# Low parts by an accumulating DMA, and four seven-product pairs in every group, in a two-layer encoder trunk

## The chip, the cores and the metric

The kernel runs on one core of a Trainium2 chip. The metric is the device time of one execution in microseconds; a run's figure is the median of several executions. Each kernel also leaves a profile of one execution, with every engine's instructions, what they waited for, and the DMA queues.

The core has a matrix engine (TensorE, "PE" in the profile), three engines for elementwise work (VectorE "DVE", ScalarE "ACT", GpSimd "POOL"), and SyncE ("SP"), which here issues nearly all loads. Each engine works through its own instructions in order.

## The reference, cut to what matters

The program is a trunk of two layers on 256 tokens of width 2048, in float32. Each layer has attention and a squared-ReLU MLP with 8192 hidden features:

```python
def sq_relu_mlp(h, g, w_in, w_out):
    return jnp.square(jax.nn.relu(rms_norm(h, g) @ w_in)) @ w_out

for layer in range(DEPTH):                 # DEPTH = 2
    ...
    h = h + jnp.concatenate([y_main, y_mem], axis=-1) @ w_o[layer]
    h = h + sq_relu_mlp(h, norm_mlp[layer], w_mlp_in[layer], w_mlp_out[layer])
```

The change touches only the second product of the MLP, the down projection: (256 x 8192) times (8192 x 2048), in both layers.

## The kernel before, in words

**Two parts of each number.** A float32 product is made of three matmuls in the engine's rounded 32-bit format (fp32r). Each operand is split into a high part, which is its rounding, and a low part, which is the rest; then high x high, high x low and low x high are added in PSUM. For weights the high part is a cast on ScalarE and the low part a subtraction on VectorE (`parts`, L173 and L176).

**Units.** All weights stream through the kernel as units of 128 x 1024 values (512 KB), in one list `stream` whose order is the order of their use. `prepare` takes the next unit: it gets a raw tile, a high tile and a low tile, loads raw with a DMA from SP, and makes the two parts. The pools hold 6 raw, 4 high and 5 low tiles. `weights` keeps up to four units prepared ahead of the one that the matmuls take. Matmuls are issued in program order; for the other engines a planner, which goes by its own costs, sets the order of the instructions within an engine.

**The MLP.** Hidden features are worked in four chunks of 2048. A chunk has an up stage (16 tiles of features, 32 units) and then down projections by tokens. In chunks 0 to 2 the 2048 output columns are covered by two pair groups of 1024 columns each; in chunk 3 by one pair group and two plain groups of 512 columns (the last of layer 1 is done by features). That is 7 pair groups a layer, 14 in all.

**A pair group** (`pair_group`) has 8 pairs of feature tiles j. A pair is a 2 x 2 block product: two halves of the tokens, two tiles of features, two sides of 512 output columns. It is done in one of two ways.

- Direct: one unit for the left side and one for the right (`Gathered`, steps "1" and "2"), each with 4 block products of 3 matmuls, 24 for the pair. The DMA gathers the unit from four rows of the weight's layout, so raw has the order (o, k, n), with o one of four runs of 128 output columns and k the feature tile. The cast (L249) and the subtraction (L250) turn it to (k, o, n), so that a matmul reads 512 columns in one run.
- By seven products (`Sevenfold`, steps 0 to 3): the scheme of Winograd and Strassen, with 7 block products instead of 8, 21 matmuls of 512 columns for the pair. Its two raw tiles stay until the fourth step; VectorE forms sums of weight blocks in place (L222, L223, L225, L226), the cast is L227 and the subtraction L228. The sums on the token side (`factors`) are made at the end of a feature tile in the up stage (`finish`, L1111 to L1125).

`SEVEN[layer][chunk][group]` says which pairs go by seven products: 9 of the 14 groups have four such pairs (0, 2, 4, 6), and 5 have three (0, 2, 4). `group_order` lays the direct units between the steps. With four seven-product pairs the order of a pair is: step 0, step 1, a direct unit, step 2, a direct unit, step 3. The group then has 8 direct units; with three it has 10.

The two plain groups of chunk 3 take `Gathered` units too (24 of them over both layers); they go through `tile_by_tokens`.

POOL does the low part of the hidden activations (L1095), some sums of squares and other small work; before the change it issues no DMA of weights.

Of the kernel before, what the change touches and what calls it, by code (L numbers as in the profile page):

```python
# [9 lines left out]
F32 = mybir.dt.float32  # L10
F32R = mybir.dt.float32r
AF = mybir.ActivationFunctionType
ALU = mybir.AluOpType
# [29 lines left out]
WARM_UP = 10  # L43


THREE, FOUR = (0, 2, 4), (0, 2, 4, 6)
SEVEN = [
    [(FOUR, FOUR), (THREE, FOUR), (THREE, FOUR), (THREE,)],
    [(FOUR, FOUR), (THREE, FOUR), (THREE, FOUR), (FOUR,)],
]  # L50


def group_order(sevens):
# [13 lines left out]
class InOrder:  # L67


    def __init__(self, tc, engine):  # L70
        self._tc, self._engine = tc, engine
# [10 lines left out]
class Gathered:  # L82


    def __init__(self, ap):
        self.ap = ap


class Sevenfold:
# [16 lines left out]
def trunk(  # L106
# [17 lines left out]
    nc = Engines(tc)  # L124
# [21 lines left out]
    for _ in range(WARM_UP):  # L146
# [9 lines left out]
        out=neg_tri[:], in_=neg_ones[:], pattern=[[-1, P]], compare_op=ALU.is_ge,  # L156
# [9 lines left out]
    stream = []  # L166
    prepared = deque()
    state = {"next": 0}

    def parts(raw, hi, lo, shared=False):  # L170

        n = 256 if shared else raw.shape[-1]
        nc.scalar.copy(hi[:, :n], raw[:, :n])  # L173
        if shared:
            nc.vector.tensor_copy(hi[:, n:], raw[:, n:])
        nc.vector.tensor_tensor(lo, raw, hi.bitcast(F32), op=ALU.subtract)  # L176
# [55 lines left out]
    def prepare():  # L232
        i = state["next"]
        if i >= len(stream):
            return
        state["next"] = i + 1
        if isinstance(stream[i], Sevenfold):
            prepare_seven(i, stream[i])
            return
        raw = raws.tile([P, 1024], F32, name=f"raw{i}", tag="raw")  # L240
        hi = his.tile([P, 1024], F32R, name=f"hi{i}", tag="hi")
        lo = los.tile([P, 1024], F32R, name=f"lo{i}", tag="lo")
        if isinstance(stream[i], Gathered):

            nc.sync.dma_start(raw[:].rearrange("p (o x) -> p o x", o=4), stream[i].ap)
            turned = raw[:].rearrange("p (o k n) -> p k o n", o=4, k=2)
            hi4 = hi[:].rearrange("p (k o n) -> p k o n", o=4, k=2)
            lo4 = lo[:].rearrange("p (k o n) -> p k o n", o=4, k=2)
            nc.scalar.copy(hi4, turned)  # L249
            nc.vector.tensor_tensor(lo4, turned, hi4.bitcast(F32), op=ALU.subtract)  # L250
            prepared.append((hi, lo))
            return
        nc.sync.dma_start(raw[:], stream[i])
        parts(raw[:], hi[:], lo[:])
        prepared.append((hi, lo))
# [33 lines left out]
    def mm(o, lhs, rhs, start, stop):  # L289
        nc.tensor.matmul(o, lhs, rhs, start=start, stop=stop)  # L290

    width = {"last": "narrow"}

    def tile_by_tokens(banks, act, unit, k2, kt, early=False):
        hi, lo = unit
        h512 = hi[:, k2 * 512 : (k2 + 1) * 512]
        l512 = lo[:, k2 * 512 : (k2 + 1) * 512]
        steps = []
        for m in range(2):
            a_hi = act[:, kt, m * P : (m + 1) * P]  # L300
            a_lo = act[:, kt, T + m * P : T + (m + 1) * P]

            steps.append((0, banks[m][:], a_hi, h512, kt == 0, False))
            steps.append((2, banks[m][:], a_hi, l512, False, False))
            steps.append((1, banks[m][:], a_lo, h512, False, kt == KT - 1))
        if early:

            steps.sort(key=lambda step: step[0])
        for step in steps:
            mm(*step[1:])  # L310
# [492 lines left out]
    def mlp_stream(l):  # L803
        for c in range(NCH):
            n = FIRST_UP if c == 0 else 0
            for h in range(2):
                for f in range(n):
                    stream.append(w_up[l, c * KT + f, h])
            for f in range(n, KT):
                for h in range(2):  # L810
                    stream.append(w_up[l, c * KT + f, h])
            def unit(g, j):
                ap = w_down[l, 4 * g : 4 * g + 4, 2 * c + j // 4]
                ap = ap[:, :, 256 * (j % 4) : 256 * (j % 4) + 256]
                return ap.rearrange("o p x -> p o x")

            for n, sevens in enumerate(SEVEN[l][c]):
                for j, step in group_order(sevens):
                    sides = [unit(2 * n + i, j) for i in range(2)]
                    if step == 0:  # L820
                        seven = Sevenfold(*sides)
                    stream.append(Gathered(sides["12".index(step)]) if step in ("1", "2") else seven)
            for g in range(2, 4) if c == NCH - 1 else ():
                if by_features(l, c, g):
                    for o in range(4 * g, 4 * g + 4):
                        for h in range(2):
                            stream.append(w_down[l, o, 2 * c + h])
                    continue
                stream.extend(Gathered(unit(g, j)) for j in range(KT // 2))
# [141 lines left out]
    def mlp(l, xg_, sq, h, done):  # L971
# [52 lines left out]
        def pair_group(c, n, hid, factors, staged=None):  # L1024

            banks = {q: ps_mm.tile([P, 512], F32, name="acc", tag="acc") for q in ("11", "21", "12", "22")}
            banks.update((q, ps_s.tile([P, 512], F32, name="acc", tag="s")) for q in ("p1", "p5"))
            banks["p6"] = ps_t.tile([P, 512], F32, name="acc", tag="t")
            banks["p7"] = ps_y.tile([P, 512], F32, name="acc", tag="y")
            sevens = len(SEVEN[l][c][n])  # L1030
            counts = {q: [0, 3 * sevens] for q in banks}
            for q in ("11", "21", "12", "22"):
                counts[q][1] = 6 * (KT // 2 - sevens) + (3 * sevens if q != "22" else 0)

            sums_of = {
                "11": [summed(0, 2 * n)], "21": [summed(1, 2 * n)],
                "12": [summed(0, 2 * n + 1)], "22": [summed(1, 2 * n + 1)],
                "p1": [product_sum(0, n), summed(0, 2 * n)], "p6": [product_sum(0, n)],
                "p5": [product_sum(1, n)], "p7": [product_sum(2, n)],
            }  # L1040

            def add(q, a, w):
                product(banks[q], a, w, counts[q])
                if counts[q][0] < counts[q][1]:
                    return
                src = banks[q][:]
                if staged is not None and q in ("12", "22", "p1", "p5", "p6", "p7"):

                    copy = wide.tile([P, 512], F32, name="copy", tag="wide")
                    nc.scalar.copy(copy[:], src)  # L1050
                    staged.extend((dst, copy[:]) for dst in sums_of[q])
                    return
                for dst in sums_of[q]:
                    if c == 0 and q not in ("11", "p6"):
                        nc.scalar.copy(dst, src)
                    else:
                        nc.vector.tensor_tensor(dst, src, dst, op=ALU.add)

            def tokens(kt, m):
                return [hid[:, kt, i * T + m * P : i * T + (m + 1) * P] for i in range(2)]  # L1060

            def part(unit, k2):
                return [x[:, k2 * 512 : (k2 + 1) * 512] for x in unit]

            for j, step in group_order(SEVEN[l][c][n]):
                w = weights()
                if step in ("1", "2"):
                    for m in range(2):
                        for k2 in range(2):
                            add(f"{m + 1}{step}", tokens(2 * j + k2, m), part(w, k2))  # L1070
                    slot()
                    continue
                s = factors[j]
                pairs = [
                    (("p1", tokens(2 * j, 0)), ("11", tokens(2 * j + 1, 0))),
                    (("12", s[3]),),
                    (("p5", s[0]), ("p7", s[2])),
                    (("p6", s[1]), ("21", tokens(2 * j + 1, 1))),
                ][step]
                for k2, (q, a) in enumerate(pairs):  # L1080
                    add(q, a, part(w, k2))
                if step in (1, 3):
                    slot()

        began = clock["slot"]
        for c in range(NCH):
# [4 lines left out]
            def finish(f, hid=hid, squares=squares, factors=factors, c=c):  # L1091
# [5 lines left out]
                )  # L1097
                if f % 2 == 0 or f // 2 not in SEVEN[l][c][-1]:
                    return
# [46 lines left out]
            n = FIRST_UP if c == 0 else 0  # L1146
# [60 lines left out]
            for g in range(2, 4):  # L1207
# [3 lines left out]
                for o in range(4 * g, 4 * g + 4):  # L1211
                    if o == KT - 1:
                        last_tile(
                            hid, lambda b, o=o: down_early(o, b), lambda b, o=o: down_last(o, b)
# [183 lines left out]
```

## Time and profile before

| | before |
|---|---|
| median of 3 runs | 2166.65 us (2166.62 to 2167.13) |
| the profiled execution: span from first to last instruction | 2165.4 us |
| TensorE busy | 2158.2 us |
| VectorE busy | 1690.1 us |
| ScalarE busy | 1191.3 us |
| POOL busy | 326.7 us |
| read from memory | 410.58 MB, 191 GB/s over the span |
| SP's queue: packets' share of 16 DMA engines | 62.0% |

The profiled execution has no time of its own beside its span; the span is 1.25 us under the median of the runs. In rows of groups, the columns are line, engine, operation, output and inputs, shapes and count, then busy time and mean duration in ns, then the idle time of the engine before them and what ended it. In rows of the timeline, the first two numbers are the start and the length in us. Matmuls overlap in the pipeline, so their single durations are longer than the distance between them.

### The profile page before, as it was taken

How to read it: one execution, taken by the hardware profiler on the slowest of the kernel's cores; microseconds unless marked ns; L12 is line 12 of the kernel's file. 1: busy time of each engine (PE TensorE's matmuls, PEld its weight loads, DVE VectorE, ACT ScalarE, POOL GpSimd, SP SyncE). 2: the span in 40 equal slices, each digit the busy share in tenths (PEclk: the TensorE clock that was granted, in tenths of full speed). 3: DMA queues.
4: the chain of work that ended last, by engine and by line, in shares of the span. 5: the costliest groups of instructions: out<-in, count | busy, mean ns of one | idle time of the engine just before them, and what ended most of it. 6: DMA issues, size and time to landing. Idle time of an engine off the chain costs nothing.

```text
span 2165.4 us, 30280 instructions
## 1 busy us (share of the span) xinstructions
PE 2158.2 (100%) x11083; PEld 1852.1 (86%) x11083; DVE 1690.1 (78%) x2431; ACT 1191.3 (55%) x1668; POOL 326.7 (15%) x349
## 2 busy tenths in 40 slices
PE   9999999999999999999999999999999999999999
PEld 8888888888888888888888889888888888988887
DVE  7778885678977987997886556567797798799796
ACT  7744545555655555555555447655565556555553
POOL 0010112621001001001050112352100100100100
PEclk9999999999999999999999999999999999999999
DMA  9655556655765765666666654455676577667665
GB/s 325 197 165 185 168 179 195 198 192 166 212 205 178 208 213 178 194 219 189 202 180 191 185 190 136 131 188 183 182 201 224 164 203 223 188 180 219 190 180 156
DMA packets 213317, 414.66 MB, mean 191 GB/s; under 512 B 13232, under 2 KB 144304, under 8 KB 213168
## 3 DMA queue, kind: packets, MB, share of 16 engines
q1 hardware_dynamic: 212592, 410.63, 62.0%
q8 instruction: 87, 1.43, 0.3%
q10 hardware_dynamic: 576, 2.10, 0.3%
q14 instruction: 62, 0.51, 0.1%
HBM read 410.58 MB, written 2.10 MB: 191 GB/s over the span
## 4 chain that ended last, share of the span: by engine, by line
PE 98%; DVE 1%; DMA 0%; issue 0%; ACT 0%; SPq 0%
PE acc L77 94%; PE yp L77 1%; PE accs L77 1%; PE tp L77 1%; PE s L77 1%; PE z L77 1%; DMA raw<-in_w_mem 0%; DVE lo L176 0%; DVE pt L640 0%; DVE lo L250 0%; DVE h L998 0%; ACT hi L173 0%; DVE kvx L465 0%; ACT hi L249 0%; PE stat L77 0%
## 5 line engine op out<-in xcount | busy, mean ns | idle before, releaser
L176 DVE TENSOR_TENSOR lo<-raw,hi 128x1024 fp32r<-128x1024 f32 (+1 forms) x524 | 642.6, 1237 | 308.4 <-ACT hi L173 183.3
L173 ACT CAST hi<-raw 128x1024 fp32r<-128x1024 f32 (+1 forms) x524 | 546.4, 1045 | 375.8 <-PE acc L77 316.7
L77 PE MATMUL acc<-hi,hid 128*128 128x512 f32 x1474 | 481.4, 389 | 0.0
L77 PE MATMUL acc<-mlpx,hi 128*128 128x512 f32 x2048 | 472.6, 390 | 0.0
L77 PEld LDWEIGHTS acc<-mlpx,hi 128*128 128x128 f32 x2048 | 382.0, 188 | 77.7
L77 PEld LDWEIGHTS acc<-hi,hid 128*128 128x128 f32 x1474 | 276.7, 188 | 57.5
L77 PE MATMUL acc<-lo,hid 128*128 128x512 f32 x737 | 286.7, 389 | 0.0
L1095 POOL TENSOR_TENSOR hid<-upsq,hid 128x256 fp32r<-128x256 f32 x128 | 122.3, 964 | 1086.2 <-ACT hid L1094 1086.2
L227 ACT CAST hi<-raw 128x1024 fp32r<-128x1024 f32 x204 | 192.1, 946 | 132.8 <-PE acc L77 56.0
L77 PEld LDWEIGHTS acc<-mlpx,lo 128*128 128x128 f32 x2048 | 250.6, 192 | 2.8
L77 PE MATMUL acc<-mlpx,lo 128*128 128x256 f32 x2048 | 252.0, 283 | 0.0
L228 DVE TENSOR_TENSOR lo<-raw,hi 128x1024 fp32r<-128x1024 f32 x204 | 222.8, 1108 | 29.6 <-ACT hi L227 28.0
L249 ACT CAST hi<-raw 128x1024 fp32r<-128x1024 f32 x146 | 154.0, 1055 | 126.1 <-PE acc L77 104.5
L77 PE MATMUL acc<-hi,xg 128*128 128x512 f32 x640 | 208.4, 398 | 0.0
L250 DVE TENSOR_TENSOR lo<-raw,hi 128x1024 fp32r<-128x1024 f32 x146 | 179.2, 1228 | 14.4 <-ACT hi L249 13.7
L77 PEld LDWEIGHTS acc<-lo,hid 128*128 128x128 f32 x737 | 138.4, 188 | 28.5
L77 PEld LDWEIGHTS acc<-hi,xg 128*128 128x128 f32 x640 | 120.2, 188 | 24.6
L451 ACT COPY low<-acc 128x256 f32<-128x256 f32 x188 | 69.1, 368 | 112.2 <-PE acc L77 111.9
L77 PE MATMUL acc<-lo,xg 128*128 128x512 f32 x320 | 124.7, 390 | 0.7 <-DVE lo L176 0.7
L77 PE MATMUL acc<-y,hi 128*128 128x512 f32 x512 | 119.9, 391 | 0.0
L77 PEld LDWEIGHTS acc<-y,hi 128*128 128x128 f32 x512 | 95.0, 188 | 19.0
L1094 ACT CAST hid<-upsq 128x256 fp32r<-128x256 f32 x128 | 51.9, 407 | 75.6 <-DVE upsq L1093 75.4
(202 smaller groups left out, 2610.4 us busy)
## 6 DMA issues: line engine op xcount, KB each, us to landing
raw<-in_w_up SPq DMA_DIRECT2D x256, 512.0 KB, 4.4
raw<-in_w_down SPq DMA_DIRECT2D x256, 512.0 KB, 5.6
raw<-in_w_in SPq DMA_DIRECT2D x80, 512.0 KB, 3.7
raw<-in_w_o SPq DMA_DIRECT2D x64, 512.0 KB, 4.0
raw<-in_w_mem SPq DMA_DIRECT2D x28, 512.0 KB, 5.9
raw<-in_w_kv_v SPq DMA_DIRECT2D x24, 512.0 KB, 3.9
raw<-in_w_kv_k SPq DMA_DIRECT2D x24, 512.0 KB, 4.2
raw<-in_w_q SPq DMA_DIRECT2D x24, 512.0 KB, 4.1
```

Source lines behind the costliest of these rows:

```text
L77: return self._tc.keep_in_program_order(fn(*args, **kwargs))
L173: nc.scalar.copy(hi[:, :n], raw[:, :n])
L176: nc.vector.tensor_tensor(lo, raw, hi.bitcast(F32), op=ALU.subtract)
L227: nc.scalar.copy(hi4, src)
L228: nc.vector.tensor_tensor(lo4, src, hi4.bitcast(F32), op=ALU.subtract)
L249: nc.scalar.copy(hi4, turned)
L250: nc.vector.tensor_tensor(lo4, turned, hi4.bitcast(F32), op=ALU.subtract)
L451: nc.scalar.copy(low[:], bank[:, T:])
L1094: nc.scalar.copy(hid[:, f, :T], a[:])
L1095: nc.gpsimd.tensor_tensor(hid[:, f, T:], a[:], hid[:, f, :T].bitcast(F32), op=ALU.subtract)
```

## The change

Direct units of the pair groups carry a mark, `by_dma`. Their low part isn't made by VectorE: ScalarE writes the rounding of -raw into the low tile, and a DMA issued from POOL adds raw onto it in place (512 KB from raw, accumulated into the low tile). The sum is raw minus the high part. `Gathered` units of the two plain groups in chunk 3 keep the subtraction on VectorE.

All `Gathered` units, marked or not, are no longer turned when they are split: high and low tiles keep the order (o, k, n), and the matmul reads its 512 columns as four runs of 128 (`turned`, `of_k`).

All 14 groups now have four seven-product pairs, so five groups exchange a direct pair for a seven-product pair. Their order of steps is then that of the other groups.

```diff
-THREE, FOUR = (0, 2, 4), (0, 2, 4, 6)
-SEVEN = [
-    [(FOUR, FOUR), (THREE, FOUR), (THREE, FOUR), (THREE,)],
-    [(FOUR, FOUR), (THREE, FOUR), (THREE, FOUR), (FOUR,)],
-]
+FOUR = (0, 2, 4, 6)
+SEVEN = [[(FOUR, FOUR), (FOUR, FOUR), (FOUR, FOUR), (FOUR,)] for _ in range(2)]
...
-    def __init__(self, ap):
+    def __init__(self, ap, by_dma=False):
         self.ap = ap
+        self.by_dma = by_dma
...
             nc.sync.dma_start(raw[:].rearrange("p (o x) -> p o x", o=4), stream[i].ap)
-            turned = raw[:].rearrange("p (o k n) -> p k o n", o=4, k=2)
-            hi4 = hi[:].rearrange("p (k o n) -> p k o n", o=4, k=2)
-            lo4 = lo[:].rearrange("p (k o n) -> p k o n", o=4, k=2)
-            nc.scalar.copy(hi4, turned)
-            nc.vector.tensor_tensor(lo4, turned, hi4.bitcast(F32), op=ALU.subtract)
-            prepared.append((hi, lo))
+            nc.scalar.copy(hi[:], raw[:])
+            if stream[i].by_dma:
+                nc.scalar.activation(lo[:], raw[:], AF.Copy, scale=-1.0)
+                nc.gpsimd.dma_start(out=lo[:].bitcast(F32), in_=raw[:], accum_op=ALU.add)
+            else:
+                nc.vector.tensor_tensor(lo[:], raw[:], hi[:].bitcast(F32), op=ALU.subtract)
+            turned = [x[:].rearrange("p (o k n) -> p k o n", o=4, k=2) for x in (hi, lo)]
+            prepared.append(turned)
             return
...
+    def of_k(x, k2):
+
+        return x[:, k2] if len(x.shape) == 4 else x[:, k2 * 512 : (k2 + 1) * 512]
...
-                    stream.append(Gathered(sides["12".index(step)]) if step in ("1", "2") else seven)
+                    stream.append(
+                        Gathered(sides["12".index(step)], True) if step in ("1", "2") else seven
+                    )
...
             def part(unit, k2):
-                return [x[:, k2 * 512 : (k2 + 1) * 512] for x in unit]
+                return [of_k(x, k2) for x in unit]
```

More of the change, by code (lines that the diff above doesn't have):

```diff
@@ L292, in trunk @@
     width = {"last": "narrow"}
+    def of_k(x, k2):
+        return x[:, k2] if len(x.shape) == 4 else x[:, k2 * 512 : (k2 + 1) * 512]
     def tile_by_tokens(banks, act, unit, k2, kt, early=False):
         hi, lo = unit
-        h512 = hi[:, k2 * 512 : (k2 + 1) * 512]
-        l512 = lo[:, k2 * 512 : (k2 + 1) * 512]
+        h512, l512 = of_k(hi, k2), of_k(lo, k2)
         steps = []
```

## The prediction

> **What bounds the kernel now.** I read the page first: busy shares and the chain that ended last.
>
> ```profile
> span 2165.4 us, 30280 instructions
> PE 2158.2 (100%) x11083; PEld 1852.1 (86%) x11083; DVE 1690.1 (78%) x2431; ACT 1191.3 (55%) x1668; POOL 326.7 (15%) x349
> ...
> PE 98%; DVE 1%; DMA 0%; issue 0%; ACT 0%; SPq 0%
> ```
>
> The chain is PE, 98% of it, and PE is without work for only 2165.4 - 2158.2 = 7.2 us. The span stands 1.25 us under the median of the runs (2166.65), so what I work out on the span carries over to the median.
>
> Then the waits of PE alone, and one piece of the chain with nothing but 512-wide products.
>
> ```profile
> PE tp L77 <- DVE h L998: 1.9, 2, 1.1
> PE cold L77 <- DVE zeros L144: 1.1, 1, 1.1
> PE acc L77 <- DVE lo L176: 0.7, 1, 0.7
> PE accs L77 <- ACT hi L173: 0.4, 1, 0.4
> ```
>
> ```profile
> 31.56 2.72 PE acc L77 x12
> ```
>
> No down projection unit is waited for today, and one 512-wide matmul costs 2.72 / 12 = 0.2267 us of PE's time (the longer durations of single matmuls overlap).
>
> Next the first two pair groups of layer 0 and the up stage behind them (PE, PEld, DVE, ACT, POOL busy, clock, DMA share, GB/s).
>
> ```profile
> 524.79:565.60 40.81, 40.81 (x182) 33.80 (x181) 39.20 (x47) 26.27 (x33) 2.95 (x2) 1.00 0.75 203
> 565.60:606.40 40.80, 40.80 (x182) 33.80 (x181) 36.90 (x41) 26.58 (x32) 0.00 (x0) 1.00 0.72 210
> 606.40:697.50 91.10, 91.10 (x524) 80.64 (x523) 67.81 (x107) 49.22 (x75) 12.44 (x15) 1.00 0.59 185
> ```
>
> A group with four seven-product pairs has 4 x 21 + 4 x 24 = 180 matmuls, and 180 x 0.2267 = 40.8 us: exactly its length. So even where VectorE is busy 36.9 of 40.8 us (90%), PE loses nothing to it. Relief of VectorE is worth nothing here by itself; what is left to win is the number of matmuls.
>
> **The part that gains.** Five groups go from three seven-product pairs to four (layer 0: one each in chunks 1, 2 and 3; layer 1: one each in chunks 1 and 2). Each replaces 24 matmuls by 21, so 15 x 0.2267 = 3.40 us leave the chain. Layer 0's chunk 3 gets factors for one more pair: four small VectorE operations, two casts, two subtractions. The dearest of these rows is
>
> ```profile
> L1111 DVE TENSOR_TENSOR s<-upsq 128x128 f32<-128x128 f32 x62 | 42.0, 718 | 1.0
> ```
>
> Eight operations at no more than 0.72 us are under 6 us once, spread over an up stage in which VectorE is busy 67.8 of 91.1 us: nothing.
>
> **The part that moves.** After the change all 14 pair groups have 8 direct units, 112 in all. Each loses a VectorE subtraction (L250) and gains a ScalarE copy with scale -1, and a DMA issued from POOL that adds 512 KB of raw onto it.
>
> ```profile
> L228 DVE TENSOR_TENSOR lo<-raw,hi 128x1024 fp32r<-128x1024 f32 x153 | 188.8, 1238 | 22.5 <-ACT hi L227 20.9
> L250 DVE TENSOR_TENSOR lo<-raw,hi 128x1024 fp32r<-128x1024 f32 x146 | 179.2, 1228 | 14.4 <-ACT hi L249 13.7
> L249 ACT CAST hi<-raw 128x1024 fp32r<-128x1024 f32 x146 | 154.0, 1055 | 126.1 <-PE acc L77 104.5 <-issue 10.6 <-DVE raw L222 6.2
> ```
>
> VectorE in a group: 36.9 - 8 x 1.23 = 27.1 us of 40.8. ScalarE: 26.6 + 8 x 1.06 = 35.0 of 40.8, taking the cast's price for the scaled copy. Both still fit, so neither is the new bound by its sum. POOL has next to nothing in a group:
>
> ```profile
> L1095 POOL TENSOR_TENSOR hid<-upsq,hid 128x256 fp32r<-128x256 f32 x128 | 122.3, 964 | 1086.2 <-ACT hid L1094 1086.2
> ```
>
> At a group's start the issue of an accumulation waits on POOL for its copy, and the last low parts of hid (L1095) queue behind it. They are token factors of the group's last pairs, wanted some 30 us later, so a few us there cost nothing; were that cover gone, it would be the waiting time itself, once a group.
>
> Direct units are also no longer turned on the way in: the matmul now reads 512 columns as four runs of 128. The trace has no such moving operand. The nearest rows:
>
> ```profile
> L77 PE MATMUL acc<-hi,hid 128*128 128x512 f32 x1474 | 481.4, 389 | 0.0
> L77 PE MATMUL acc<-hi,xg 128*128 128x512 f32 x640 | 208.4, 398 | 0.0
> ```
>
> I take no cost; the spread between forms, 9 ns, on 12 matmuls of all 136 gathered units (1632) would be 15 us, and below nothing there is no reason for a gain, since PE already runs at one pitch in all forms. ScalarE and VectorE reading straight instead of turned: L249 and L250 cost today what straight ones cost (1.055 against L228's neighbours, 1.228 against 1.238), so nothing.
>
> **What decides: the time from a copy to its landed sum.** A low tile has five buffers, a high tile four. In the steady middle of the second group one pair takes 10.2 us and goes s0, s1, D1, s2, D2, s3 (s: seven-product steps, D: direct units; 6, 3, 12, 6, 12, 6 matmuls). PE, then ScalarE, then VectorE, then SP's loads of direct units:
>
> ```profile
> 588.25 0.39 PE L77 MATMUL acc<-hi,hid 128*128 128x512 f32 x1
> 588.48 0.39 PE L77 MATMUL acc<-lo,hid 128*128 128x512 f32 x1
> ```
>
> ```profile
> 582.33 0.62 ACT L227 CAST hi<-raw 128x512 fp32r<-128x512 f32 x1 [0.26 <-PE acc L77]
> 585.05 1.05 ACT L249 CAST hi<-raw 128x1024 fp32r<-128x1024 f32 x1 [2.10 <-PE acc L77]
> 586.45 1.06 ACT L227 CAST hi<-raw 128x1024 fp32r<-128x1024 f32 x1 [0.35 <-PE acc L77]
> ```
>
> ```profile
> 577.68 1.22 DVE L228 TENSOR_TENSOR lo<-raw,hi 128x1024 fp32r<-128x1024 f32 x1
> ...
> 585.41 0.69 DVE L225 TENSOR_TENSOR raw<-raw,raw 128x512 f32<-128x512 f32 x1
> 586.14 1.23 DVE L250 TENSOR_TENSOR lo<-raw,hi 128x1024 fp32r<-128x1024 f32 x1
> ```
>
> ```profile
> 577.19 2.10 SPq L245 DMA_DIRECT2D raw<-in_w_down  x2
> ...
> 587.39 2.10 SPq L245 DMA_DIRECT2D raw<-in_w_down  x2
> ```
>
> D1's second matmul reads its low tile at 588.48. Today VectorE delivers it at 586.14 + 1.23 = 587.37, 1.1 us ahead. After: its low buffer comes free when PE has done the unit five before, the previous s2, at 588.25 - 0.68 - 1.36 - 1.36 - 2.72 = 582.13. The scaled copy reads only raw, not the high tile, so it may go before the cast that waits at 585.05 for a high buffer. I take it that it does: in the rows, L225 of the pair's last step runs ahead of L250, which stands earlier in the code, so the planner does move ready work ahead. Then the copy ends at about 582.2 + 1.06 = 583.3, or at 584.0 if it goes behind the 0.62 us cast of 582.33, and the sum must have landed by 588.48: a budget of 5.1 us at best, 4.4 us in the present order. D2 has the same distance (6.12 us of matmuls between the unit five before and itself), and a stall at D1 counts for D2 too. So a pair pays once: the landing time less the budget.
>
> The landing time of an accumulation, counted from the end of the copy and with POOL's issue in it, stands in no row. The nearest are these:
>
> ```profile
> raw<-in_w_in SPq DMA_DIRECT2D x80, 512.0 KB, 3.7
> ...
> out_t<-h SPq DMA_DIRECT2D x16, 128.0 KB, 1.8
> DMA to landing us min/median/max: 4.2/5.4/7.7
> ```
>
> ```profile
> DMA  9655556655765765666666654455676577667665
> GB/s 325 197 165 185 168 179 195 198 192 166 212 205 178 208 213 178 194 219 189 202 180 191 185 190 136 131 188 183 182 201 224 164 203 223 188 180 219 190 180 156
> ```
>
> Lower end: 3.7 us, the quickest kind of 512 KB load (a 128 KB store takes 1.8). Upper end: the longest landing of L245, 7.7, plus its median again for the second operand, 13.1. An addition has to fetch both operands. I take the median of the direct units' own loads under the same traffic, 5.4, and for the extra 512 KB the rate of the busiest slice, 524 KB / 325 GB/s = 1.6 us: 7.0 us. It is nearer the lower end because both operands lie on the core.
>
> Sum: 7.0 - 5.1 = 1.9 us a pair, 14 groups x 4 pairs = 56, so 106 us of new waits; less 3.4. **Forecast: 2166.65 + 106 - 3.4 = 2269 us.** With 4.4 us of budget and 7.7 us of landing it is 56 x 3.3 - 3.4 = 181 more (2348), with 5.8 (the shortest landing, 4.2, plus 1.6) and 5.1 it is 56 x 0.7 - 3.4 = 36 more (2202). SP's loads go out the moment a raw tile is free (587.39, behind D1's L250); afterwards a direct unit's raw is held until its sum has landed, which pushes in the same direction, as SP's queue is in order and the next pair's loads stand behind.
>
> **Rivals.** First, all of it hidden. If the accumulation lands within 5.1 us (3.7 to 5.1), PE waits for nothing, and what stays is 3.4 us: 2163.2. For it: the budget lies inside the bounds, and POOL's queue is empty. Against it: the median of today's landings alone is 5.4. It comes out under 2162.3 only if about 1 us of the 7.2 us of PE's idle time goes too (down to 2156 at most). The Trainium skill, "DMA: Bandwidth & Descriptors", section "Anatomy of one DMA", gives for DMAs issued from GpSimd a fixed 2.0 us plus bytes over 436 GB/s. An estimate from that page, with 1 MB read for 512 KB written, is 4.4 us, so by that rule the time is 2163; the trace's own loads (5.4 against the page's 3.2 for 512 KB) are slower than the rule, and no run here shows an accumulation.
>
> Second, the DMA engines become the bound, not the latency. In a group 16 loads take 0.73 x 40.8 = 29.8 us of all engines, 1.86 each, and 11.0 us are free for 8 accumulations, 1.4 us each. At 1.86 each a group gets 44.7 us long, at twice that 59.6: 14 x 3.9 = 55 us to 14 x 18.8 = 263 us more, so 2218 to 2426. For it: the DMA share of 0.72 to 0.75. Against it: those loads are gathered in rows of 1 KB from far memory, and the share counts the time packets are under way. The Trainium skill, "Collectives: The Full Stack", section on why ReduceScatter is half of AllGather, says that a sum in the DMA path reads two sources and runs at about half a copy's rate; no row here shows it, and by it the upper figure holds.
>
> Third, the planner puts the copy behind the cast. Then D1's copy ends at 585.05 + 1.05 + 1.06 = 587.2, the budget is 1.3 us, and a pair pays 5.7: 56 x 5.7 - 3.4 = 316, 2482. For it: that is the order in the code. Against it: L225.
>
> **How the numbers follow.** Latency, as forecast: 0.45. Hidden: 0.33, of it 0.09 under 2162.3. Engines: 0.12. Copy behind the cast: 0.10. About 0.2% (4.3 us) is what a measurement of this kernel can tell from no change: faster by more 0.09, within 0.24, slower 0.67. The range takes in the hidden case at 2163 and the engines' case to its end: 2161 to 2420, leaving out the third rival, the upper tail and a sliver below. The likeliest case's own range is 2200 to 2350.
>
> **What the changed profile would show.** Forecast right: PE's waits gain a row "acc <- DMA lo" of some 100 us in some 56 to 112 pieces, PE's busy share falls to about 95%, and the group windows are 48 us long with POOL's queue holding issues. Hidden: PE's list of waits as now, windows of 40.8 us everywhere. Engines: a DMA share near 1 in those windows, landings of loads well over 5.4, and waits for hi as much as for lo. Copy behind cast: on ScalarE each scaled copy stands right behind its L249 cast. In every case VectorE loses 122 subtractions of 1.23 us and gains the pairs' own, and a pitch other than 0.2267 us in direct units would show the runs of 128 to cost. The prediction is wrong if accumulations land in 5 us or less, or if groups lengthen with lo landed in time.

## The result, and the profile after

The changed kernel takes 2523.42 us (median of 4 runs, 2517.23 to 2526.15) against 2166.86 us of the kernel before: a ratio of 1.1642, 95% interval 1.1625 to 1.1658. The sign of the forecast is right, its size is not: 357 us were lost where 102 were forecast, and the time lies above the range.

The page of the changed kernel: span, busy times, PE's granted clock over the span, the queue of the accumulations (packets, MB, share of 16 engines), the chain that ended last, and the row of the accumulation (count, KB, median us to landing).

```profile
span 2523.0 us, 30772 instructions
PE 2288.1 (91%) x11068; PEld 1926.0 (76%) x11068; DVE 1597.9 (63%) x2355; ACT 1302.8 (52%) x1792; POOL 421.0 (17%) x461
...
PEclk9999999997998899899899999999889889988989
...
q0 software_dynamic: 16128, 58.73, 12.1%
...
PE 75%; DMA 17%; issue 3%; DVE 2%; ACT 2%; POOL 0%; ACTq 0%; POOLq 0%
...
lo<-raw POOLq DMA_DIRECT2D x112, 512.0 KB, 7.0
```

Its waits of PE (total us, times, longest), the largest row:

```profile
PE acc L74 <- DMA lo<-raw: 224.1, 67, 6.5
```

Two things grew. PE stands idle 2523.0 - 2288.1 = 234.9 us, against 7.2 before. And PE is **busy** 129.9 us longer (2288.1 against 2158.2) with 15 matmuls fewer, mainly because the clock is no longer full. Together they are the 357.6 us between the spans. Over 56 pairs (14 groups of 4) that is 4.07 us of idle time and about 2.3 us of slower matmuls each.

Two pairs of the second group of layer 0, in the view by windows (after the busy times: granted clock, DMA share, GB/s). Each window is one pair long, from some 6 us behind one wait to the same point behind the next:

```profile
577.20:594.20 17.00, 12.98 (x46) 10.16 (x46) 7.41 (x9) 10.17 (x14) 1.71 (x2) 0.80 0.76 187
594.20:611.80 17.60, 12.91 (x47) 10.18 (x46) 7.88 (x10) 8.26 (x10) 1.72 (x2) 0.81 0.74 179
```

A pair took 10.2 us before; now it takes about 17, with every engine less busy than the window is long, and the DMA share where it was (0.72 to 0.75 before). Over a pair nothing is full; the time is a latency. Within a pair it is uneven:

```profile
598.15:605.40 7.25, 2.58 (x12) 1.80 (x10) 5.82 (x7) 3.28 (x4) 1.72 (x2) 0.86 0.96 224
603.40:610.10 6.70, 4.68 (x11) 3.72 (x12) 1.58 (x3) 0.00 (x0) 0.00 (x0) 0.50 0.91 239
610.20:620.30 10.10, 7.93 (x35) 6.19 (x33) 4.97 (x6) 7.58 (x8) 1.35 (x2) 1.00 0.62 151
```

While the accumulation that PE waits for is under way (598.15 to 605.40) the DMA share is 0.96, with the loads that go out at the same time. And the granted clock is 0.50 from 603.40 to 610.10, which begins inside PE's wait, and 1.00 behind that.

The timeline of the same group, PE first. The bracket is idle time and what ended it.

```profile
605.41 0.79 PE L74 MATMUL acc<-lo,hid 128*128 128x512 f32 x1 [4.69 <-DMA lo<-raw]
606.01 1.05 PE L74 MATMUL acc<-hi,hid 128*128 128x512 f32 x2
...
606.86 0.63 PE L74 MATMUL acc<-lo,hid 128*128 128x512 f32 x1
...
610.21 0.40 PE L74 MATMUL acc<-hi,s_hi 128*128 128x512 f32 x1
...
617.74 0.39 PE L74 MATMUL acc<-hi,hid 128*128 128x512 f32 x1
622.22 0.80 PE L74 MATMUL acc<-lo,hid 128*128 128x512 f32 x1 [4.09 <-DMA lo<-raw]
```

Then ScalarE and POOL between the two waits:

```profile
611.85 1.05 ACT L225 CAST hi<-raw 128x1024 fp32r<-128x1024 f32 x1 [0.34 <-PE acc L74]
612.80 1.06 ACT L246 ACTIVATE lo<-raw 128x1024 fp32r<-128x1024 f32 x1
613.76 1.03 ACT L244 CAST hi<-raw 128x1024 fp32r<-128x1024 f32 x1
```

```profile
614.15 0.86 POOL L247 DMA_DIRECT2D lo<-raw  x1 [10.88 <-DVE lo L226]
```

This is the whole story of a pair, from wait to wait, 622.22 - 605.41 = 16.81 us. Both waits stand at the second matmul of a pair's second direct unit; the first direct unit between them (613.66 to 616.15) waits for nothing.

| step | ends at | us |
|---|---|---|
| the other 11 matmuls of the second direct unit | 610.21 | 4.80, where 11 x 0.2267 = 2.49 |
| the fourth step, 6 matmuls at 0.2267; a low buffer comes free | 611.57 | 1.36 |
| to the next start on ScalarE | 611.85 | 0.28 |
| that is a cast of a seven-product step (L225); the copy stands behind it | 612.80 | 0.95 |
| the scaled copy (L246) | 613.86 | 1.06 |
| POOL's issue | 614.15 | 0.29 |
| the accumulation lands, PE goes on | 622.22 | 8.07 |

(POOL's row names a subtraction on VectorE as releaser; it and the copy end within 0.3 us of each other.) The 11 slow matmuls are 4.80 / 11 = 0.436 us apart, about half the pace, and the first and third rows of PE above show the same: 605.41 to 606.86 is 1.45 us for three. After them the pitch is 0.2267 again.

### The profile page after: what moved, and what is told of

Read it like the earlier page. It is cut to its first block, busy times and chain, and to the rows that moved or that the text cites. A ratio compares the mean times of both kernels' runs of the same rounds, so it can differ in the third digit from the quotient of the medians.

```text
span 2523.0 us, 30772 instructions
## 1 busy us (share of the span) xinstructions
PE 2288.1 (91%) x11068; PEld 1926.0 (76%) x11068; DVE 1597.9 (63%) x2355; ACT 1302.8 (52%) x1792; POOL 421.0 (17%) x461
## 4 chain that ended last, share of the span: by engine, by line
PE 75%; DMA 17%; issue 3%; DVE 2%; ACT 2%; POOL 0%; ACTq 0%; POOLq 0%
PE acc L74 71%; DMA lo<-raw 17%; DVE lo L226 1%; ACT hi L225 1%; PE accs L74 1%; PE yp L74 1%; PE tp L74 1%; PE s L74 1%; PE z L74 1%; ACT lo L246 1%; POOL lo L247 0%; PE cold L74 0%; DVE lo L174 0%; DVE pt L643 0%; ACT low L454 0%
## 5 line engine op out<-in xcount | busy, mean ns | idle before, releaser
L74 PE MATMUL acc<-hi,hid 128*128 128x512 f32 x1424 | 542.8, 446 | 0.0
L74 PE MATMUL acc<-lo,hid 128*128 128x512 f32 x712 | 332.6, 467 | 224.1 <-DMA lo<-raw 224.1
L226 DVE TENSOR_TENSOR lo<-raw,hi 128x1024 fp32r<-128x1024 f32 x224 | 240.5, 1090 | 388.1 <-ACT hi L225 388.0
L74 PEld LDWEIGHTS acc<-lo,hid 128*128 128x128 f32 x712 | 159.3, 224 | 287.2 <-DMA lo<-raw 252.8
L74 PEld LDWEIGHTS acc<-hi,hid 128*128 128x128 f32 x1424 | 316.9, 223 | 71.5
L244 ACT CAST hi<-raw 128x1024 fp32r<-128x1024 f32 x136 | 142.2, 1045 | 365.6 <-PE acc L74 360.7
L225 ACT CAST hi<-raw 128x1024 fp32r<-128x1024 f32 x224 | 210.8, 942 | 92.8 <-PE acc L74 43.5
L247 POOL DMA_DIRECT2D lo<-raw x112 | 97.0, 866 | 752.4 <-ACT lo L246 357.4
L246 ACT ACTIVATE lo<-raw 128x1024 fp32r<-128x1024 f32 x112 | 118.2, 1055 | 6.3 <-DMA raw<-in_w_down 6.2
```

Source lines behind the costliest of these rows:

```text
L74: return self._tc.keep_in_program_order(fn(*args, **kwargs))
L225: nc.scalar.copy(hi4, src)
L226: nc.vector.tensor_tensor(lo4, src, hi4.bitcast(F32), op=ALU.subtract)
L244: nc.scalar.copy(hi[:], raw[:])
L246: nc.scalar.activation(lo[:], raw[:], AF.Copy, scale=-1.0)
L247: nc.gpsimd.dma_start(out=lo[:].bitcast(F32), in_=raw[:], accum_op=ALU.add)
```

## The experiments

The kernel before, run again beside them, had medians of 2166.49 to 2166.95 us.

**1. The change without the DMA, and the new split alone.** All units keep VectorE's subtraction in the changed kernel; and the kernel before gets four seven-product pairs in every group, its turned layout kept.

```diff
-  Gathered(sides["12".index(step)], True) if step in ("1", "2") else seven
+  Gathered(sides["12".index(step)], False) if step in ("1", "2") else seven
```

> The changed kernel, but VectorE makes the low parts of all direct units again; four seven-product pairs in every group and the unturned layout stay. Theory (the accumulation's time from free buffer to landed sum is the whole loss): PE waits for no low part, every matmul of a direct unit stays at 0.2267 us, 15 matmuls fewer than before: 2163.4, at most 2170. Rival (part of the 357 us comes from moving operands read as four runs of 128, or from VectorE being full in the five exchanged groups): 2180 or more, with a pitch above 0.2267 us or waits for VectorE in those groups.

> The kernel before with one edit: four seven-product pairs in every group. All low parts by VectorE, direct units turned. Theory: 2166.9 - 15 x 0.2267 = 2163.4, since groups of this kind lost nothing before. Rival: VectorE at 90% of a group doesn't keep up in the five exchanged groups and PE waits there: 2167 or more. Its distance to the run with unturned units by VectorE is the price of the four runs of 128: 0 by the theory, up to 15 us by the rival.

Measured: 2173.11 us (1.0029 [1.0018, 1.0041]) and 2172.88 us (1.0028 [1.0017, 1.0038]). The two differ by 0.2 us, so reading 512 columns as four runs of 128 costs nothing. And four seven-product pairs with VectorE's low parts are not 3.4 us faster but some 6 us slower. The exchanged group of layer 0, chunk 1, in the view by windows, first of the kernel before, then of the first experiment, there with the start of the group behind it:

```profile
695.40:736.90 41.50, 41.50 (x184) 34.36 (x183) 38.56 (x46) 22.48 (x25) 2.81 (x2) 1.00 0.70 203
```

```profile
694.95:735.75 40.80, 40.80 (x182) 33.79 (x181) 39.85 (x48) 24.05 (x27) 2.95 (x2) 1.00 0.70 197
735.75:745.00 9.25, 7.78 (x32) 5.59 (x31) 9.15 (x12) 4.50 (x5) 0.00 (x0) 1.00 0.41 113
```

In the exchanged group VectorE goes from 93% to 98% of the window, and PE still loses nothing. But VectorE leaves the group with work undone, and PE waits for it in the first pair of the next group, 1.5 us in three pieces, of which this is the longest:

```profile
742.93 0.50 PE L74 MATMUL acc<-lo,s_hi 128*128 128x512 f32 x1 [0.94 <-DVE lo L226]
```

The same three waits stand in four places, behind the exchanged groups of chunks 1 and 2 of both layers. From chunk 1 on, VectorE also adds nearly all the sums that leave PSUM (nine such instructions in this group); each of the two groups of chunk 0 that I had read has only two of them:

```profile
727.22 0.69 DVE L1062 TENSOR_TENSOR e<-acc,e 128x512 f32<-128x512 f32 x1
```

**2. Everything of the change but the accumulation.** The scaled copy stays, the DMA goes; the low part stays the negated rounding.

```diff
-  nc.gpsimd.dma_start(out=lo[:].bitcast(F32), in_=raw[:], accum_op=ALU.add)
```

> The changed kernel without the accumulating DMA: the low part of a direct unit stays the negated rounding (wrong values); the second copy on ScalarE, the unturned layout and four seven-product pairs everywhere are all there. Theory (the landing alone makes the loss, and VectorE's relief is real): no wait for low parts, clock 1.0, and the 15 matmuls saved come out: 2163 to 2165. Rival (the second copy on ScalarE, behind casts that wait for high buffers, is late by itself, as the waits left with a sixteenth of the bytes allow): 2180 to 2270.

Measured: 2163.31 us (2162.65 to 2163.89), 0.9984 [0.9975, 0.9993]. Page and the second group of layer 0 by windows:

```profile
PE 2154.3 (100%) x11068; PEld 1848.1 (85%) x11068; DVE 1596.3 (74%) x2355; ACT 1300.8 (60%) x1792; POOL 324.8 (15%) x349
```

```profile
565.60:606.40 40.80, 40.80 (x182) 33.78 (x181) 28.54 (x33) 32.96 (x39) 0.00 (x0) 1.00 0.70 207
```

The clock is full, VectorE has fallen to 28.5 and ScalarE risen to 33.0 of 40.8 us (27.1 and 35.0 forecast), and the 3.4 us of fewer matmuls are there. So the accumulation makes the whole loss, and if its sums came for nothing the change would be worth its 3.4 us. Against the 2154.3 us of PE here, the 2288.1 of the changed kernel are 133.8 us more for the same matmuls. Both traces hold the same 11068 matmuls in the same order, so they can be set side by side: the last one of the changed kernel ends 356.8 us later, of which 226.6 are idle time at the waits, 115.6 lie in stretches with a recorded clock of 0.5 (57 of them, 314 us in all), and 14.6 are matmuls drawn out right at a wait or behind it. So of the 133.8 us some 116 are the clock.

**3. Is the slow clock made by the idle time?** The wait of each second direct unit is filled with 18 matmuls of 0.2267 us, which alters the values.

```diff
+  fill["n"] = 18 if fill["unit"] % 2 == 0 else 0
...
+  while fill["n"]:
+      fill["n"] -= 1
+      mm(bank[:], neg_tri_r[:], w[0], False, False)
```

> The changed kernel, with 18 more matmuls (512 columns, weights of a constant triangle, added into the same bank, so the down projection's values are altered) right behind the first matmul of every second direct unit of a pair group, where PE waits some 4 us: 56 x 18 = 1008 matmuls, 4.1 us a pair. Theory (a third of the loss, some 130 us, is PE running at half clock after each wait, because it stood idle): the granted clock stays at 1.0, the waits are filled, and the time falls to 2370 to 2430 although 1008 matmuls are added. Rival (the slow matmuls have another cause, such as the accumulation's traffic): the clock in the groups stays near 0.81 and the time stays at 2520 or rises.

Measured: 2475.1 us (2465.3 to 2482.0), 1.1419 [1.1395, 1.1443]. Page, then PE's waits:

```profile
PE 2412.8 (97%) x12076; PEld 2039.7 (82%) x12076; DVE 1600.2 (65%) x2355; ACT 1303.4 (53%) x1792; POOL 420.9 (17%) x461
```

```profile
PE acc L74 <- DMA lo<-raw: 50.7, 40, 3.1
```

The fillers are 12076 - 11068 = 1008 matmuls, 228.5 us. The rest of PE's work is 2412.8 - 228.5 = 2184.3 us, 30 over the 2154.3 of full clock where the changed kernel had 133.8. So idleness makes the slow clock: with PE kept at work about 100 us of it go, and the mean granted clock is 0.996 instead of 0.938. The time fell by 48 us only, less than expected: filler and idle time (2475.1 - 2412.8 = 62.3) are 291 us together, 56 more than the changed kernel's idle time, and an accumulation landed in 7.4 instead of 7.0 us. Why the latency grew by about 1 us a pair was not followed further.

**4. What the landing consists of.** A plain copy in place of the sum; the sum for 64 of 1024 columns only; and the plain copy issued from ScalarE's queue in place of POOL's.

```diff
-  nc.gpsimd.dma_start(out=lo[:].bitcast(F32), in_=raw[:], accum_op=ALU.add)
+  nc.gpsimd.dma_start(out=lo[:].bitcast(F32), in_=raw[:])
...
+  nc.gpsimd.dma_start(
+      out=lo[:, :64].bitcast(F32), in_=raw[:, :64], accum_op=ALU.add
+  )
...
+  nc.scalar.dma_start(out=lo[:].bitcast(F32), in_=raw[:])
```

> The changed kernel, with the DMA from POOL copying raw over the low tile instead of adding to it (the low parts of direct units are then raw itself, so the values are wrong): same bytes written, same queue, same issue, but one operand read instead of two. Theory (the second operand is part of the landing time): landing falls from 7.0 to about 5.5 us, each pair waits some 1.5 us less, 84 us in all, and more if the clock recovers: 2380 to 2450. Rival (the queue and the fixed part of a DMA from POOL decide, the addition is free): landing stays near 7 us and the time near 2523.

> The changed kernel, with the accumulation done for 64 of the 1024 columns only (the rest of the low part stays the negated rounding, so the values are wrong). Copies, issues on POOL and waits are all there; a sixteenth of the bytes moves. Theory (the landing is mostly transfer, so a short one fits the budget of some 5 us): it lands in 2 to 3.5 us, PE waits for nothing, the clock stays at 1.0, and with VectorE relieved the 15 matmuls saved come out: 2160 to 2167. Rival (a DMA from POOL has a large fixed time, or the copies and issues on ScalarE and POOL are late by themselves): landing above 5 us, or waits remain, and the time stays above 2250.

> The plain copy of raw over the low tile once more (one operand, wrong values), but issued from ScalarE's queue, right behind the scaled copy there, not from POOL's. Theory (a landing is transfer and waiting behind loads on the same 16 engines, whoever issues): landing 5.2 to 5.7 us as with POOL's issue, less only the time of POOL's issue, and 2330 to 2390. Rival (the software queue of POOL is the slow part): landing 3 to 4 us and under 2260.

| kernel | us | ratio | median landing | engines' time each | PE idle | PE busy |
|---|---|---|---|---|---|---|
| changed kernel | 2523.42 | 1.1642 [1.1625, 1.1658] | 7.0 | 2.73 | 234.9 | 2288.1 |
| plain copy, POOL | 2383.39 | 1.0984 [1.0957, 1.1011] | 5.7 | 1.34 | 161.9 | 2228.4 |
| plain copy, ScalarE | 2327.12 | 1.0741 [1.0727, 1.0756] | 4.9 | shares its queue |  117.4 | 2208.0 |
| sum of a sixteenth | 2274.19 | 1.0498 [1.0483, 1.0514] | 4.8 | 0.39 | 85.3 | 2188.1 |

Engines' time is the time that a transfer's packets took, spread over 16 engines: the queue's share times the span, by 112. For the plain copy and the sixteenth, queue and landing (first the copy, then the sixteenth):

```profile
q0 software_dynamic: 16128, 58.73, 6.3%
...
DMA to landing us min/median/max: 2.9/5.7/8.7
```

```profile
q0 software_dynamic: 16128, 3.68, 1.9%
...
DMA to landing us min/median/max: 2.1/4.8/7.6
```

The addition doubles the engines' time of a transfer (2.73 against 1.34 us) and adds 1.3 us to the landing; issuing from ScalarE saves 0.8 us, and its 4.9 us lie between the two expectations. The Trainium skill, "Collectives: The Full Stack", on why ReduceScatter is half of AllGather, says that a sum in the DMA path reads two sources and runs at about half a copy's rate; the trace agrees. But a sixteenth of the bytes still lands in 4.8 us, where 2 to 3.5 were expected: most of the 7.0 us are not the transfer's own bytes. The times of the packets in the traces say where they are. In the changed kernel the first packet of an accumulation starts a median of 2.4 us behind the issue (1.4 at least), the packets are under way for 4.1 us (2.8 at least), and 0.3 us later the sum has landed; with a sixteenth of the bytes the first two are 2.7 (1.4 at least) and 1.5 (0.4 at least). That the time above the least values is queueing behind the loads fits this, but no run took the loads away. In every row a shorter landing takes slow matmuls away with the idle time.

**5. Can the distance be made longer?** Direct units get two low buffers of their own, so that a copy doesn't wait for a buffer that a seven-product step holds; seven-product steps share three, and units outside the pair groups take from both. A control has the same buffers and no DMA.

```diff
+  own = i % 5 in (1, 3) if not isinstance(stream[i], Gathered) else stream[i].by_dma or i % 5 in (1, 3)
+  tag = "lo_d" if own else "lo"
+  lo = los.tile([P, 1024], F32R, name=f"lo{i}", tag=tag, bufs=2 if own else 3)
```

> The changed kernel, with the five low buffers divided: two for direct units alone, three for the rest (units of other phases use both, in turn). A direct unit's buffer then comes free at the end of the direct unit two before it, 7.48 us of matmuls ahead instead of 6.12. Theory (the distance from the free buffer to the need decides): each pair waits 1.4 us less, and up to 2.4 us more is saved where the clock recovers: 2523 - 76 = 2447, down to 2310; the three buffers of the other units may take some of it back. Rival (the DMA engines decide): no change, 2510 to 2530.

> Control for the split of the low buffers (three and two, units in turn), with no accumulation at all: four seven-product pairs everywhere, VectorE makes every low part. If the split costs nothing: as the all-VectorE run, 2173. If a unit now meets a buffer that is still in use: up to 2190, with waits for low parts in up stages as well.

Measured: 2342.53 us (1.0817 [1.0795, 1.0838]) with the DMA, 2181.31 us (1.0067 [1.0055, 1.008]) without. PE's idle time falls from 234.9 to 2344.0 - 2214.7 = 129.3 us, 1.9 us a pair. Freeing the buffer earlier takes away half of the loss; the split itself costs 8.2 us (2181.31 against 2173.11). With the pairs closer together the DMA share rises, in a stretch of the same group almost to 1:

```profile
600.00:620.00 20.00, 19.43 (x82) 15.37 (x80) 10.67 (x13) 12.21 (x14) 3.45 (x4) 0.97 0.96 256
```

More low tiles beside the full five were not tried.

**6. Fewer accumulations.** Only the first direct unit of each pair goes by DMA (56 of 112); that with buffers of its own; and that in the five exchanged groups alone (20).

```diff
+  direct += step in ("1", "2")
...
+  Gathered(sides["12".index(step)], direct % 2 == 1) if step in ("1", "2") else seven
```

> The changed kernel, with only the first direct unit of each pair by DMA (56 accumulations), the second by VectorE. Latency theory: one chain a pair is left, its copy stands behind one short cast, traffic is less and the landing about 6 us: 0.1 + 0.62 + 1.06 + 0.3 + 6.0 = 8.1 us against 6.35, so 1.7 us a pair, 56 x 1.7 = 98 us on 2163: 2260, up to 2330 with a slowed clock. Rival (the engines' load decides, 29.8 + 8 x 2.73 = 51.6 us in a group of 40.8 before and 29.8 + 4 x 2.73 = 40.7 now): it just fits, 2163 to 2200.

> Two edits together: two low buffers for accumulated units alone (three for the rest), and only the first direct unit of each pair by DMA. Such a unit's buffer then comes free two pairs before its next use, 2 x 10.2 - 2.72 = 17.7 us ahead, against some 8.5 us from copy to landing. Latency theory: no wait for a landed sum is left, the clock stays at 1.0, VectorE has 4.9 us less in each group, and the matmuls saved come out: 2160 to 2172. Rival (DMA engines: 29.8 + 4 x 2.73 = 40.7 us in a group of 40.8, so loads are late now): waits for raw or for landed sums remain, 2200 to 2300.

> As the run with two own buffers and the first direct unit of a pair by DMA, but only in the five groups that went from three to four seven-product pairs, where VectorE alone costs 9.4 us (2173 against 2163.4); 20 accumulations in all. Latency theory: VectorE catches up there and no landed sum is late: 2163 to 2167. Rival (a late sum at the start of each group, or the split of the buffers, costs as much): 2170 to 2185.

Measured: 2348.87 us (1.0845 [1.0823, 1.0867]); 2329.01 (1.0741 [1.0724, 1.0757]); 2229.35 (1.0288 [1.0274, 1.0303]), 48 us above the control of experiment 5, 2.4 us for each accumulation. All three missed what was expected. I had thought the wait gone once the only accumulation of a pair had a low buffer waiting for it; the timeline of the second kernel shows what took its place, on PE, on SP's queue, on ScalarE, on POOL and on PE again:

```profile
581.04 0.50 PE L74 MATMUL acc<-lo,hid 128*128 128x512 f32 x1 [2.25 <-DMA lo<-raw]
...
594.88 0.80 PE L74 MATMUL acc<-lo,hid 128*128 128x512 f32 x1 [3.07 <-DMA lo<-raw]
```

```profile
581.05 0.92 SPq L245 DMA_DIRECT2D raw<-in_w_down  x2
```

```profile
586.16 1.06 ACT L248 ACTIVATE lo<-raw 128x1024 fp32r<-128x1024 f32 x1 [5.48 <-DMA raw<-in_w_down]
```

```profile
587.51 0.85 POOL L249 DMA_DIRECT2D lo<-raw  x1 [13.79 <-ACT lo L248]
```

An accumulation reads raw until it has landed. The moment it lands (581.04) SP issues the next loads (581.05); these take 5.11 us to the copy, the copy 1.06, the issue 0.29, the landing 7.37: 13.84 us, which is the distance of PE's two waits, against 10.2 us of work in a pair. The **raw** tile closes a circle of its own, and it is longer than a pair even with one accumulation in it.

**7. Where the way from buffer to need is longer.** In the plain groups direct units stand in a row, and a low buffer comes free 10.9 us of matmuls ahead. Only the 24 units of the plain groups go by DMA, the pair groups by VectorE.

```diff
+  Gathered(sides["12".index(step)], False) if step in ("1", "2") else seven
...
-  stream.extend(Gathered(unit(g, j)) for j in range(KT // 2))
+  stream.extend(Gathered(unit(g, j), True) for j in range(KT // 2))
```

> The accumulation is moved to where direct units stand in a row: the 24 units of the plain groups of the last chunk get their low parts by DMA, the 112 of the pair groups by VectorE. There the unit five before ends 4 x 2.72 = 10.9 us ahead. Latency theory: copy 1.06, issue 0.3, landing 7 to 8 us, at most one cast ahead, 1.06: 8.4 to 10.4 us, so PE waits for nothing or for under 1 us a group, and the time is that of the all-VectorE run within 5 us. Rival (the DMA engines are full: 12.1% of 2523 us over 112 accumulations is 2.73 us of all engines each): 8 loads and 8 accumulations take 8 x (1.86 + 2.73) = 36.7 us where 8 units take 21.8, so each of the three groups gets some 15 us longer, 45 us in all, 2205 to 2215.

Measured: 2203.97 us (1.0172 [1.0158, 1.0185]), 30.9 us over the first experiment. The plain groups of layer 0 by windows (with the end of the pair group ahead of them), the landings of the 24 accumulations, and the landings of the loads in this window:

```profile
1076.00:1127.00 51.00, 37.35 (x151) 29.65 (x149) 20.85 (x27) 27.40 (x32) 19.08 (x24) 0.87 1.04 255
```

```profile
DMA to landing us min/median/max: 7.8/9.4/13.7
...
DMA to landing us min/median/max: 6.8/13.0/19.3
```

Here the DMA share is 1.04 and loads land in a median of 13.0 us: the engines are full, as the second rival had it. In the two pairs of the changed kernel shown above the share was 0.74 and 0.76, and its direct units' loads land in a median of 5.5 us (5.4 before). PE waits for landed sums for 12.3 us over the whole run, and once for something else:

```profile
PE tp L74 <- DVE h L1003: 8.6, 2, 7.8
```

The wait of 7.8 us, 1.1 without the DMA, begins on ScalarE: it stands 6.71 us at a copy whose raw tile is still loading, work for later products (L466) stands behind that copy, VectorE waits for this work, and PE for VectorE.

## Why the prediction was partly right

**Right.** The sign; that the changed landing is what decides, and that nothing else in the change costs (experiment 2); that in the steady middle of a group PE waits once a pair, at a low part (though at the second direct unit, where the prediction reckoned with the first), and that ScalarE, VectorE and POOL fit by their sums; that the new matmul operand costs nothing (experiment 1); the landing's median, 7.0 us from the issue, as estimated from the loads' landing and the busiest slice (the estimate was to hold the 0.29 us up to the issue as well); that the planner puts the copy ahead of the same unit's cast (612.80 and 613.76), so the third rival falls in the form it was given.

**Wrong: the term "landing less budget", 1.9 us a pair, 106 in all.** It measured 4.07 us a pair, 227.7 in all. The last part of the way was the one I had: buffer free, copy, landing. Between these I left out three things, and the pair at 605 to 622 us prices them. By my reckoning the copy ended 0.2 + 1.06 us after the buffer was free and the sum landed 7.0 us later, 8.2 us in all against 6.35 to the second matmul. In the trace 0.28 and 0.95 us go by ahead of the copy, as ScalarE takes a cast of *another* unit that becomes ready at the same moment, released by the same matmuls; I had asked only whether the copy passes its own cast, and had put the cost of an order with one cast ahead at 0.7 us, for the range. Then 0.29 us to the issue and 8.07 us to the landing, 1.36 over the 7.0 that were to hold both. It is 10.65 us, and 10.65 - 6.35 = 4.3 of wait (4.09 in the bracket). A median over all accumulations is the wrong figure for the ones that PE stands waiting for: in the trace the 66 whose landing ends a wait of PE took a median of 7.8 us, the other 46 took 6.3.

**Wrong: a term that was missing.** PE's work was taken to cost 0.2267 us a matmul whatever happens around it. After a wait of 4 us the next 11 run at 0.436. Slower matmuls make 133.8 us, over a third of the loss, some 116 of it under a clock of 0.5, and experiment 3 shows idleness as the cause. The trace of before could not show it: PE's waits there were of 1.1 us and less. The Trainium skill, "TensorE: Matmul & The Clock Gate", section "HAM oscillation — how this bites in real kernels", describes it: a loop whose matmuls wait 3 to 5 us for a DMA in each turn runs the next turn at half clock. The trace agrees, and this page was the rule to weigh: my 1.9 us of wait lay below its window of about 3.4 us, the range's upper case of 3.3 us did not lie clear of it, and its price was left out of the upper end. In the runs even 1.9 us was not safe: waits of 1.79 to 1.93 us in the changed kernel were followed by the slow pitch.

**Wrong: the 3.4 us, as an argument.** "PE loses nothing" to a VectorE at 90% was read in chunk 0 and carried to the five exchanged groups, which lie in chunks 1 to 3, where VectorE has other sums to add. With VectorE's low parts the exchange costs 6 us more instead of 3.4 less; the waits come in the group behind an exchanged one, as VectorE is late there. The term itself stood: with VectorE relieved it is 3.4 us (experiment 2). So the relief was not worth nothing; it is what four seven-product pairs need.

**Half seen: the raw tile.** "Pushes in the same direction" had no number. While the low buffer decided it cost little; once that was eased (experiment 6) it alone kept a pair at 13.84 us.

**The rivals.** Hidden: no; accumulations landed in 4.5 to 10.5 us, median 7.0. The estimate of 4.4 us worked out from the Trainium skill, "DMA: Bandwidth & Descriptors", section "Anatomy of one DMA", lay under every landing of the changed kernel. Engines full: not over the pair groups of the changed kernel, where the latency made room, though the share is near 1 while a late sum is under way (0.96 from 598.15 to 605.40), so that full engines lengthen the landing there is not ruled out; it holds in the plain groups (experiment 7). (Its upper figure, 2426, lay 6 us beyond the end of the range that was said to take it in.) And it stands next in line: 29.8 us of engines' time for a group's loads, by the prediction's count, and 8 x 2.73 = 21.8 for its accumulations are 51.6, more than the 40.8 us of the group, and the 0.96 of experiment 5 points the same way. How far the latency and how far the engines hold the pairs there stays open.

No kernel here computes the reference faster than the one before.

## What to carry to other kernels

When a result is moved from an engine to a DMA, count the round trip of the buffers that it holds, from the matmul that frees a tile to the matmul that needs the next one, with each instruction that becomes ready at the same moment put ahead of it once, and compare that with the work in one turn; every tile held until the landing (here low and raw) closes a circle of its own. Take the landing from the transfers that someone waits for, under the stage's own load, not from a median of all. A wait of some 2 us or more on TensorE can cost more than itself: price the matmuls behind it at half clock as well.

## What the runs showed of the hardware that I had not expected

- Half clock after short waits: behind PE's waits of 4.02 to 4.69 us in the second group of layer 0 the matmuls ran at about half pace for some 4.8 us, under a recorded clock of 0.5. The bound is not sharp: 1.79 us in the changed kernel and 2.27 us in the kernel with a sixteenth of the sum were followed by the slow pitch, while 2.25 us in the kernel with own buffers and one accumulation a pair, and 3.69 us in the one without the own buffers, were not. The Trainium skill, "TensorE: Matmul & The Clock Gate", section "Part 1: The HAM clock gate (the "warmup" mystery)", says that the window of about 3.4 us runs free, which fits such a spread.
- The size of an accumulation sets only a part of its landing under load: 4.8 us for 32 KB, 7.0 for 512 KB.
- A sum inside a DMA takes the engines 2.73 us for 512 KB between tiles on the core, a plain copy 1.34; it lands 1.3 us later, and a copy issued from POOL 0.8 us later than one from ScalarE.
